# A matmul with rotary embedding: earlier turns of tiles 5 to 7, and other cuts of the last output units

## The chip, the cores and the metric

The kernel runs on one core of one Trainium2 chip. The metric is the device time of one execution in microseconds. The engines are TensorE (PE, with its weight loads listed as PEld), VectorE (DVE), ScalarE (ACT), GpSimd (POOL) and SyncE (SP), which here issues DMAs.

## The reference

For x of 16 x 512 x 768, a weight of 768 x 768, and cos and sin of 512 x 64, all float32, with 12 heads of 64:

```
y = matmul(x, weight).reshape(batch, seq, 12, 64)
y1, y2 = y[..., :32], y[..., 32:]
out1 = y1 * cos[:, :32] - y2 * sin[:, :32]
out2 = y2 * cos[:, 32:] + y1 * sin[:, 32:]
out = concatenate([out1, out2], -1).reshape(batch, seq, 768)
```

## The kernel before, in words

The 16 x 512 rows make 64 tiles of 128 rows, counted from 0 in this document. Four tiles make a group; there are 16 groups, 0 to 15 (`LAST` is 15). A group's output has 4 x 768 = 3072 columns and fills six PSUM banks of 512 columns (`py`, keys `ps0` to `ps5`). Two more banks (`pt`, two buffers) take the transposes.

A tile goes through these steps. SP loads it (`load`, L205) into one of ten buffers `xs`. ACT casts it to float16 (`cast`, L185, one of five buffers `xc`). PE turns it, that is, transposes it chunk by chunk into `pt`, and ACT copies `pt` into SBUF (`xt`, L185 again). There are two kinds of turn: `turn` (L251) uses one `pt` buffer and six transposes of 128 x 128; `turn_rows` (L266) turns the two halves of the partitions apart, twelve transposes of 64 x 64, and uses both `pt` buffers. From the first tile of the main loop on, `turn_rows` is used until near the end. Ten pairs of tiles in groups 5 to 14 (`BLOCKS`) are instead turned by DVE, some of them loaded by POOL's DMA queue.

Group 0 is computed chunk by chunk as the weights arrive (`mm0`, L333). In groups 1 to 14 the contraction is cut into two row halves that run on PE side by side (`walk`, `both`, `one`, L358): half 0 visits the three banks of a pair of tiles in the order 0, 1, 2 and half 1 in the order 2, 0, 1, each a lag of 1024 columns behind; so bank 0 is finished first, then bank 2, and bank 1 last. The last group uses whole matmuls again (L333), unit by unit.

A finished unit of columns goes to `rope`: DVE multiplies it from PSUM with cos and with the signed sin (L410) into two product rows, and POOL adds these, with halves exchanged, into the output buffer `ov` (L427). Up to group 13's first half POOL adds 1536 columns at once; afterwards unit by unit. The last two units of 256 are added by DVE itself, after all its products. Stores (L448) go out over ACT's or SP's queue.

`units(g)` says how a group's columns are cut: 512, 1024, 512, 1024 up to group 14; in group 15 three units of 512 and six of 256, the last two of which lie in the `pt` banks. The order of all this is written out by hand and each engine works in that order; waits are derived from which tile is read and written (`Flow.do`). Calls of `casts`, `turns`, `bturns`, `pool_loads` in the main loop say how far ahead of the matmuls a tile is cast and turned (`C_AHEAD`, `T_AHEAD`). `pump`, called after each cast, issues the next loads.

Around the start of the main loop the order is: the matmuls of tile 3 (its chunks 0 to 2), turn 4, cast 6, chunks 3 to 5 of tile 3, the last product of group 0, turn 5; then, in the loop, group 1 by `both`, with turn 6, casts 7 and 8, turn 7 at the end of the step of tile 5, and cast 9.

Of the kernel before, what the change touches and what calls it, by code (L numbers as in the profile page):

```python
# [16 lines left out]
class Flow:  # L17
# [24 lines left out]
    def do(self, e, make, reads=(), writes=(), dma=None, tick=True, after=0):  # L42
        need = {}
        for k in reads:
            for s, v in self.wrote.get(k, {}).items():
                need[s] = max(need.get(s, 0), v)
        for k in writes:
            for d in (self.wrote, self.readby):
                for s, v in d.get(k, {}).items():
                    need[s] = max(need.get(s, 0), v)  # L50
        if e == "pe":
            need.pop("pe", None)
            if after:
                need["pe"] = after
        waits = self.settle(e, need)
        for s, v in waits[:-1]:
            self.eng[e].wait_ge(self.sem(s), v)
        i = make(self.eng[e])
        if waits:
            s, v = waits[-1]  # L60
            i.wait_op(self.sem(s), v, "sem-ge")
        name, step = (dma, 16) if dma else (e, 1)
        self.sem(name)
        at = self.count[name] + step
        if tick or dma:
            i.then_inc(self.sems[name], step)
            self.count[name] = at
            self.known[name, at] = dict(self.seen[e])
        for k in reads:
            d = self.readby.setdefault(k, {})  # L70
            d[name] = max(d.get(name, 0), at)
        for k in writes:
            self.wrote[k] = {name: at}
            self.readby[k] = {}
        return i
# [30 lines left out]
def kernel(  # L106
# [23 lines left out]
    QB = 4  # L130
    NG = B * SB // QB
    NTILE = QB * NG
    CHUNKS = [(t, e) for t in range(NT) for e in range(2)]
    LAST = NG - 1
# [28 lines left out]
    def products(at, n, lo, hi):  # L163

        mem, base, name = (tq_mem, at, "tq") if at < 6144 else (w_flat, at - 6144, "tw")
        keys = {f"{name}{c // 256}" for j in range(2)
                for c in range(base + j * n + lo, base + j * n + hi, 256)}
        v = mem[:, base : base + 2 * n].rearrange("p (j n) -> p j n", j=2)
        return v[:, :, lo:hi], sorted(keys)
# [3 lines left out]
    py = nc.alloc_psum_tensor("py", [P, 6 * 512], FP32).ap()  # L173
# [4 lines left out]
    def ring(name, n, state={}):  # L178
        k = state.get((id(f), name), 0)
        state[id(f), name] = k + 1  # L180
        return k % n
# [118 lines left out]

    def units(g):
        if g < LAST:
            return [(c, z, py[:, c:z], [f"ps{b}" for b in range(c // 512, z // 512)], "pool")
                    for c, z in ((0, 512), (512, 1536), (1536, 2048), (2048, 3072))]
        u = [(c, c + 512, py[:, c : c + 512], [f"ps{c // 512}"], "pool")
             for c in range(0, 1536, 512)]
        if g == LAST:
            for k, (home, bank) in enumerate([
                (py[:, 1536:1792], "ps3"), (py[:, 0:256], "ps0"),
                (py[:, 2048:2304], "ps4"), (py[:, 2560:2816], "ps5"),  # L310
                (pt_b[0][:, 0:256], "pt0"), (pt_b[1][:, 0:256], "pt1"),
            ]):
                c = 1536 + 256 * k
                u.append((c, c + 256, home, [bank], "pool" if k < 4 else "dve"))
        return u

    def pieces(g, s):
# [51 lines left out]
    at = [0, LAG]  # L369
# [22 lines left out]
    def rope(g, u):  # L392
        c0, c1, ps, banks, adder = u
        w, r = c1 - c0, g % SB
        nh = w // D
        whole = 0 < g < LAST - 1 and (g, c0 // 1536) != (LAST - 2, 1)
        if adder == "dve":
            k = len(late)
            tq, keys = xs_b[k][:, 0 : 2 * w].rearrange("p (j n) -> p j n", j=2), [f"xs{k}"]
        elif 0 < g < LAST:  # L400
            lo = c0 % 1536
            if lo == 0:
                tq_of[0] = HOMES[ring("tq", len(HOMES))]
            tq, keys = products(tq_of[0], 1536, lo, lo + w)
            if tq_of[0] >= 6144:
                keys = keys + W_HOME
        else:
            homes = HOMESL if g else HOMES0
            tq, keys = products(homes[ring(f"tq{g}", len(homes))], w, 0, w)
        do("dve", lambda eng: eng.tensor_tensor(  # L410
            out=tq.rearrange("p j (h d) -> p j h d", d=D),
            in0=ps.rearrange("p (h d) -> p h d", d=D)
            .unsqueeze(1).broadcast_to((P, 2, nh, D)),
            in1=csn[:, :, r, :].unsqueeze(2).broadcast_to((P, 2, nh, D)),
            op=MULT), reads=banks + ["csn"], writes=keys)
        if g not in ov_of:
            ov_of[g] = ring("ov", NOV)
        o = ov_of[g]

        if whole:  # L420
            if c0 % 1536 == 0:
                return
            c0, w = c0 - 512, 1536
            tq, keys = products(tq_of[0], 1536, 0, 1536)

        def add():
            do(adder, lambda eng: eng.tensor_tensor(  # L427
                out=ov_b[o][:, ds(c0, w)].rearrange("p (h t d) -> p h t d", t=2, d=HD),
                in0=tq[:, 0].rearrange("p (h t d) -> p h t d", t=2, d=HD),
                in1=tq[:, 1].rearrange("p (h t d) -> p h t d", t=2, d=HD)[:, :, ::-1, :],  # L430
                op=ADD), reads=[q for q in keys if q not in W_HOME], writes=[f"ov{o}c{c}" for c in range(c0, c1, 64)])

        if adder == "dve":
            late.append(add)
        else:
            add()
# [77 lines left out]
    def mm0(i, c):  # L514
        last = c == CHUNKS[-1]
        ps = pieces(0, i)
        for p in ps:
            a, z, _, bank = p
            stop = last and (z % 512 == 0)
            mm_piece(i, p, c, False, stop, tick=last or p is ps[-1])  # L520
# [44 lines left out]
    def casts(upto, most=NTILE):  # L565
        while state["cast"] < min(upto, NTILE) and most > 0:
            most -= 1
            i = state["cast"]
            state["cast"] += 1
            if not is_block(i):  # L570
                castx(i, "act")
            elif i % 2 == 0 and BLOCKS[pair_of(i)] == "sp":
                cast_pair(pair_of(i))
                xb_used[0] += 1
            pump()

    def turns(upto, most=NTILE):
        while state["turn"] < min(upto, NTILE) and most > 0:
            i = state["turn"]
            state["turn"] += 1  # L580
            if not is_block(i):
                most -= 1
                (turn_rows if rows_on[0] else turn)(i, "act")
# [19 lines left out]
    for g in range(LAST):  # L603
        for h in (0, 2):
            i = QB * (g + 1) + h
# [5 lines left out]
            elif g < LAST - 2:  # L611
                i = QB * (LAST - 2) + 2 * (g - LAST + 4) + h // 2
# [2 lines left out]
            stores.setdefault(i, []).append(q)  # L615

    C_AHEAD, T_AHEAD, B_AHEAD, P_AHEAD = 5, 3, 4, 20
    SETTLED = 2 * QB

    for i in (0, 1):  # L620
        mm0(i, CHUNKS[5])
# [5 lines left out]
    for c in CHUNKS[:3]:  # L627
        mm0(3, c)
    turns(5)
    casts(7)  # L630
    for c in CHUNKS[3:]:
        mm0(3, c)
    rope(0, U0[3])
    turns(6)

    for i in range(QB, NTILE):
        g, s = divmod(i, QB)
        us = units(g)
        done_to = (s + 1) * H
        rows_on[0] = QB <= i < QB * LAST - 1  # L640
        if g < LAST:
            if s % 2 == 0:
                for r in range(2):
                    lines[r].extend(walk(i // 2, r))
            for n in range(1, 4):
                both((i - QB) * 4608 + n * 1536)
                if n == 1 and i > QB + 1:
                    turns(i + T_AHEAD, 1)
        if i == QB * LAST:
            both(NTILE * 4608)  # L650
        for p in pieces(g, s) if g == LAST else ():
            a, z, _, bank = p
            for c in CHUNKS:
                mm_piece(i, p, c, c == CHUNKS[0], c == CHUNKS[-1],
                         tick=c == CHUNKS[-1])
            for u in us:
                if u[1] == z:
                    rope(g, u)
        bturns(i + B_AHEAD)
        turns(i + 1 + (T_AHEAD if i > QB + 1 else 2), 1)  # L660
        casts(i + 1 + (C_AHEAD if i >= SETTLED else 4), 2 if i == QB else 1 + i % 2)
        pool_loads(i + P_AHEAD)
        for q in stores.get(i, ()):
            store(*q)
        if g == LAST:
            if s == 2:
                store(g, 0, H, "sp")
            if s == 3:
                store(g, H, 2 * H, "act")
# [4 lines left out]
    for k, add in enumerate(late):  # L674
        c = 3 * H + 256 + 256 * k
# [38 lines left out]
```

## Time and profile before

| what | value |
|---|---|
| median of 3 runs | 153.49 us (153.34 to 154.13) |
| the profiled execution | 154.31 us |
| its span in the trace | 152.5 us |
| DMA | 51.27 MB, 336 GB/s in the mean |
| PE's granted clock | 1.00 until 140 us, 0.87 in the stretch after |

The span is the time between the first and the last event in the trace; the execution's own time has 1.8 us around it. Busy lines give the engine, its busy time and share, and its number of instructions. In a timeline line come the start, the length, the engine, the line of code, the operation with output and input tiles, shapes and count, and in brackets the idle time just before and what ended it. "DVE tq" and "DVE w_raw" are products, in one of two places in memory. A wait for several semaphores is put down to the one that came last by the profile, which can be another than the one really needed.

### The profile page before, as it was taken

How to read it: one execution, taken by the hardware profiler on the slowest of the kernel's cores; microseconds unless marked ns; L12 is line 12 of the kernel's file. 1: busy time of each engine (PE TensorE's matmuls, PEld its weight loads, DVE VectorE, ACT ScalarE, POOL GpSimd, SP SyncE). 2: the span in 40 equal slices, each digit the busy share in tenths (PEclk: the TensorE clock that was granted, in tenths of full speed). 3: DMA queues.
4: the chain of work that ended last, by engine and by line, in shares of the span. 5: the costliest groups of instructions: out<-in, count | busy, mean ns of one | idle time of the engine just before them, and what ended most of it. 6: DMA issues, size and time to landing. Idle time of an engine off the chain costs nothing.

```text
span 152.5 us, 4394 instructions
## 1 busy us (share of the span) xinstructions
PE 141.1 (93%) x1944; PEld 116.9 (77%) x1944; DVE 126.4 (83%) x92; ACT 77.5 (51%) x92; POOL 123.1 (81%) x68
## 2 busy tenths in 40 slices
PE   6869988999999999999999999999999999999910
PEld 2435656888888988888898888888888888876800
DVE  0245988588888889899989998999989998979990
ACT  3444749679877852648261906183345626362000
POOL 1000395899789997999999999999996979998990
PEclk9999999999999999999999999999999999999995
DMA  4999999999999999999999999999999999965474
GB/s 131 330 387 402 402 401 389 267 342 349 324 364 346 313 351 359 300 361 350 350 357 361 382 309 356 370 391 319 360 367 413 413 373 395 377 250 216 194 285 142
DMA packets 27555, 51.27 MB, mean 336 GB/s; under 512 B 7184, under 2 KB 13072, under 8 KB 27536
## 3 DMA queue, kind: packets, MB, share of 16 engines
q1 hardware_dynamic: 14592, 27.92, 53.5%
q10 hardware_dynamic: 7504, 21.10, 35.3%
q0 software_dynamic: 5440, 1.97, 10.4%
q8 instruction: 15, 0.25, 0.6%
q14 instruction: 4, 0.03, 0.1%
HBM read 27.79 MB, written 25.17 MB: 347 GB/s over the span
## 4 chain that ended last, share of the span: by engine, by line
PE 75%; DMA 5%; DVE 5%; POOL 4%; SPq 4%; issue 2%; ACT 2%; POOLq 0%; ACTq 0%; DVEq 0%
PE py L358 69%; DMA sin_sb<-in_sin_dram 5%; PE pt L266 5%; POOL ov L427 4%; DVE tq L410 3%; SPq L227 2%; DVE w_raw L410 2%; SPq L205 1%; ACT xc L185 1%; ACT xt L185 1%; POOLq L670 0%; SPq L464 0%; PE pt L251 0%; DVE csn L552 0%; DVE csn L554 0%
## 5 line engine op out<-in xcount | busy, mean ns | idle before, releaser
L427 POOL TENSOR_TENSOR ov<-tq 128x1536 f32<-128x1536 f32 (+3 forms) x31 | 76.6, 2487 | 19.7 <-DVE tq L410 19.7
L358 PE MATMUL py<-w_sb,xt 64*128 64x256 f16 (+1 forms) x864 | 81.9, 323 | 1.3 <-DVE tq L410 0.7
L410 DVE TENSOR_TENSOR tq<-py,csn 128x1024 f32<-128x1024 f32 (+2 forms) x47 | 74.6, 1622 | 6.4 <-PE py L358 6.2
L358 PEld LDWEIGHTS py<-w_sb,xt 64*128 64x128 f16 x864 | 62.7, 94 | 10.1 <-DVE tq L410 1.1
L185 ACT COPY xt<-pt 128x768 f16<-128x768 f16 x42 | 33.6, 800 | 53.0 <-PE pt L266 48.8
L358 PE MATMUL py<-w_sb,xp 64*128 64x512 f16 (+1 forms) x480 | 47.6, 323 | 0.0
L185 ACT CAST xc<-xs 128x768 f16<-128x768 f32 x44 | 38.7, 905 | 9.2 <-DMA xs<-in_x_dram 9.1
L410 DVE TENSOR_TENSOR w_raw<-py,csn 128x1024 f32<-128x1024 f32 (+1 forms) x20 | 35.0, 1751 | 5.1 <-PE py L358 5.0
L427 POOL TENSOR_TENSOR ov<-w_raw 128x1536 f32<-128x1536 f32 (+2 forms) x11 | 34.8, 3168 | 5.3 <-DVE w_raw L410 5.3
L358 PEld LDWEIGHTS py<-w_sb,xp 64*128 64x128 f16 x480 | 35.5, 94 | 4.5
L333 PE MATMUL py<-w_sb,xt 128*128 128x256 f16 (+1 forms) x96 | 15.5, 313 | 1.4 <-DVE w_sb L185 1.1
L266 PE MATMUL pt<-ident,xc 64*128 64x64 f16 x432 | 15.0, 190 | 0.0
L266 PEld LDWEIGHTS pt<-ident,xc 64*128 64x128 f16 x432 | 14.4, 95 | 0.8
L333 PEld LDWEIGHTS py<-w_sb,xt 128*128 128x128 f16 x96 | 8.7, 98 | 6.8 <-DVE w_sb L185 2.7
L220 POOL DMA_DIRECT2D xh<-in_x_dram x20 | 11.6, 588 | 0.0
L185 ACT CAST xd<-xb 128x1536 f16<-128x1536 f32 x5 | 8.2, 1636 | 0.0
L185 DVE CAST w_sb<-w_raw 128x768 f16<-128x768 f32 x6 | 3.3, 558 | 4.0 <-DMA w_raw<-in_weight_dram 4.0
L294 DVE STREAM_TRANSPOSE xp<-xh 128x768 f32<-128x768 f32 x5 | 6.2, 1236 | 0.0
L509 PE MATMUL py<-cold 128*128 128x512 f16 x12 | 4.9, 569 | 1.4 <-DVE cold L452 1.4
L185 DVE COPY xt<-pt 128x768 f16<-128x768 f16 x2 | 1.1, 558 | 5.2 <-PE pt L251 5.2
L251 PEld LDWEIGHTS pt<-ident,xc 128*128 128x128 f16 x48 | 3.2, 103 | 2.6 <-ACT xc L185 1.5
L294 DVE STREAM_TRANSPOSE xp<-xd 128x768 f32<-128x768 f32 x5 | 4.8, 968 | 0.0
(16 smaller groups left out, 14.4 us busy)
## 6 DMA issues: line engine op xcount, KB each, us to landing
out_dram<-ov ACTq DMA_DIRECT2D x26, 768.0 KB, 9.1
xs<-in_x_dram SPq DMA_DIRECT2D x44, 384.0 KB, 15.2
xb<-in_x_dram SPq DMA_DIRECT2D x20, 192.0 KB, 17.6
out_dram<-ov SPq DMA_DIRECT2D x4, 768.0 KB, 3.7
w_raw<-in_weight_dram SPq DMA_DIRECT2D x6, 384.0 KB, 7.6
xh<-in_x_dram POOLq DMA_DIRECT2D x20, 96.0 KB, 13.2
out_dram<-ov SPq DMA_DIRECT2D x1, 384.0 KB, 2.3
out_dram<-ov ACTq DMA_DIRECT2D x1, 384.0 KB, 2.3
```

What stands on the lines that cost most here:

```text
L185: eng.copy(out=o, in_=i_) if e == "act" else eng.tensor_copy(out=o, in_=i_)
L205: do(e, lambda eng: eng.dma_start(out=xs_b[k], in_=x[b].rearrange("(p r) h -> r p h", r=SB)[r]), writes=[f"xs{k}"], dma=f"xs{k}")
L220: do(e, lambda eng: eng.dma_start(out=dst[ts(q, R)], in_=src[r, q]), writes=[f"{name}q{q}"], dma=name)
L227: do(e, lambda eng: eng.dma_start(out=w_raw[:, t, h], in_=wv[t, h]), writes=[f"wr{t}{h}"], dma=f"w{t}{h}")
L251: do("pe", lambda eng: eng.transpose(pt[:, t, h, :], src[:, t, h, :], ident), reads=[f"xc{c}", "ident"], writes=[f"pt{k}"], tick=(t, h) == ...
L266: do("pe", lambda eng: eng.transpose(pts[r][:, t, h, :], src[rows, t, h, :], ident[rows, rows]), reads=[f"xc{c}", "ident"], writes=[f"pt{r ...
L294: do("dve", lambda eng: eng.transpose(out=dst, in_=src), reads=rd, writes=[f"xp{z}"])
L333: do("pe", lambda eng: eng.matmul(ps, get(t, h), w_sb[:, t, h, a - s * H : z - s * H], start=start, stop=stop), reads=[key, f"w{t}{h}"], w ...
L358: do("pe", lambda eng: eng.matmul(py[:, a:z], get(t, h)[rows], w_sb[rows, t, h, a - s * H : z - s * H], start=start, stop=not opens and en ...
L410: do("dve", lambda eng: eng.tensor_tensor(out=tq.rearrange("p j (h d) -> p j h d", d=D), in0=ps.rearrange("p (h d) -> p h d", d=D) .unsque ...
L427: do(adder, lambda eng: eng.tensor_tensor(out=ov_b[o][:, ds(c0, w)].rearrange("p (h t d) -> p h t d", t=2, d=HD), in0=tq[:, 0].rearrange(" ...
L509: do("pe", lambda eng: eng.matmul(py[:, ts(b, 512)], cold[:, 0:P], cold, start=True, stop=warmed[0] < WARM - 6), reads=["cold"], writes=[f ...
```

## The change

Three things. First, the order around the main loop's start: turn 5 moves ahead of tile 3's chunk 5; casts 6 and 7 follow group 0's last product; turn 6 stays at the end of the loop's first step, followed by cast 8 alone; turn 7 moves to the first third of the step of tile 5, and turn 8 takes the place at its end, followed by casts 9 and 10. Up to tile 14 each cast is then one step ahead of before; later the order is the same. Second, group 14's last unit of 1024 columns becomes two of 512, which `both` hands to `rope` as their banks are finished, bank 5 before bank 4. Third, group 15 has four units of 512 and four of 256: the columns 1536 to 2048 are one unit in bank 3 instead of two in banks 3 and 0. POOL adds the first six units, DVE the last two as before.

```
     def units(g):
         if g < LAST:
+            cut = [2560] if g == LAST - 1 else []
+            at = [0, 512, 1536, 2048] + cut + [3072]
             return [(c, z, py[:, c:z], [f"ps{b}" for b in range(c // 512, z // 512)], "pool")
-                    for c, z in ((0, 512), (512, 1536), (1536, 2048), (2048, 3072))]
+                    for c, z in zip(at, at[1:])]
         u = [(c, c + 512, py[:, c : c + 512], [f"ps{c // 512}"], "pool")
-             for c in range(0, 1536, 512)]
+             for c in range(0, 2048, 512)]
         if g == LAST:
             for k, (home, bank) in enumerate([
-                (py[:, 1536:1792], "ps3"), (py[:, 0:256], "ps0"),
                 (py[:, 2048:2304], "ps4"), (py[:, 2560:2816], "ps5"),
                 (pt_b[0][:, 0:256], "pt0"), (pt_b[1][:, 0:256], "pt1"),
             ]):
-                c = 1536 + 256 * k
-                u.append((c, c + 256, home, [bank], "pool" if k < 4 else "dve"))
+                c = 2048 + 256 * k
+                u.append((c, c + 256, home, [bank], "pool" if k < 2 else "dve"))
...
     turns(5)
-    casts(7)
-    for c in CHUNKS[3:]:
+    for c in CHUNKS[3:5]:
         mm0(3, c)
+    turns(6)
+    mm0(3, CHUNKS[5])
     rope(0, U0[3])
-    turns(6)
+    casts(8)
...
                 both((i - QB) * 4608 + n * 1536)
-                if n == 1 and i > QB + 1:
+                if n == 1 and i > QB:
                     turns(i + T_AHEAD, 1)
...
-        turns(i + 1 + (T_AHEAD if i > QB + 1 else 2), 1)
-        casts(i + 1 + (C_AHEAD if i >= SETTLED else 4), 2 if i == QB else 1 + i % 2)
+        turns(i + 1 + (T_AHEAD if i > QB else 2), 1)
+        casts(i + 1 + (C_AHEAD if i > QB else 4), 1 + i % 2)
```

More of the change, by code (lines that the diff above doesn't have):

```diff
@@ L617 @@
     C_AHEAD, T_AHEAD, B_AHEAD, P_AHEAD = 5, 3, 4, 20
-    SETTLED = 2 * QB
     for i in (0, 1):
```

## The prediction

> **What bounds the kernel now.** I read the page first: the busy shares and the chain that ended last.
>
> ```profile
> PE 141.1 (93%) x1944; PEld 116.9 (77%) x1944; DVE 126.4 (83%) x92; ACT 77.5 (51%) x92; POOL 123.1 (81%) x68
> PE 75%; DMA 5%; DVE 5%; POOL 4%; SPq 4%; issue 2%; ACT 2%; POOLq 0%; ACTq 0%; DVEq 0%
> ```
>
> PE is the bound from about 20 us on; the chain runs through its matmuls from 20.20 to 137.3 us, with one break by ACT near 22 to 25 us. After PE's last group it passes to DVE, POOL and a store. So a gain can come from PE's holes near the start or from the work after 137.3 us. Next I took the waits of PE alone, and the timelines of PE and ACT between 17 and 26 us.
>
> ```profile
> 18.27 0.50 PE L251 MATMUL pt<-ident,xc 128*128 128x128 f16 x6
> 18.73 0.80 PE L358 MATMUL py<-w_sb,xt 64*128 64x512 f16 x3
> 20.20 1.67 PE L358 MATMUL py<-w_sb,xt 64*128 64x512 f16 x16 [0.67 <-DVE tq L410]
> ...
> 24.01 0.73 PE L358 MATMUL py<-w_sb,xt 64*128 64x256 f16 x6
> 25.35 0.37 PE L358 MATMUL py<-w_sb,xt 64*128 64x512 f16 x1 [0.61 <-ACT xt L185]
> ```
>
> ```profile
> 18.46 0.89 ACT L185 CAST xc<-xs 128x768 f16<-128x768 f32 x1
> 19.25 0.81 ACT L185 COPY xt<-pt 128x768 f16<-128x768 f16 x1
> 22.09 0.80 ACT L185 COPY xt<-pt 128x768 f16<-128x768 f16 x1 [2.04 <-PE pt L266]
> 22.79 1.71 ACT L185 CAST xc<-xs 128x768 f16<-128x768 f32 x2
> ```
>
> I count tiles from 0. The four ACT lines are cast 6, copy 5, copy 6, and casts 7 and 8; copy 7 follows at 24.40 and ends at 25.21. There are two holes in PE. The second (0.61 by the profile) is the wait for copy 7, which stands behind casts 7 and 8 on ACT. The first is put down to DVE, but the first matmul of tile 5 needs bank 2, whose product (DVE's second) ended at 19.03, and copy 5, which ended at 20.06. Matmuls start 0.14 after the copy in both places (20.06 to 20.20, 25.21 to 25.35), so I read the first hole as ACT's too. Matmul ends are modelled, so I measure holes from starts: 512 columns are issued every 0.21, so the next start was due at 19.37 and came at 20.20 (0.83); at the second it was due at 24.57 and came at 25.35 (0.78).
>
> Last, the tail, from the timelines of DVE and POOL:
>
> ```profile
> 135.55 1.22 DVE L410 TENSOR_TENSOR w_raw<-py,csn 128x1024 f32<-128x1024 f32 x1 [0.27 <-PE py L358]
> 137.41 2.29 DVE L410 TENSOR_TENSOR w_raw<-py,csn 128x2048 f32<-128x2048 f32 x1 [0.63 <-PE py L358]
> ```
>
> ```profile
> 137.92 1.27 POOL L427 TENSOR_TENSOR ov<-w_raw 128x512 f32<-128x512 f32 x1
> 139.78 2.36 POOL L427 TENSOR_TENSOR ov<-w_raw 128x1024 f32<-128x1024 f32 x1 [0.58 <-DVE w_raw L410]
> 142.10 6.82 POOL L427 TENSOR_TENSOR ov<-tq 128x512 f32<-128x512 f32 x7
> ```
>
> DVE waits 0.63 for the last bank of group 14, POOL waits 0.58 for that product of 1024 columns, and then POOL works without a hole to 148.93. Its last store lands at 150.80; DVE's last store (add ended at 148.35) lands at 150.41.
>
> **The change, part by part, early.** All is rescheduled by hand with the durations of these rows; the order on each engine is read off the built instructions of both kernels.
>
> Turn 5 moves ahead of the last two matmuls of tile 3: its transposes start at 17.95 (cast 5 ended at 17.88) instead of 18.27, and copy 5 now precedes cast 6, so it starts when copy 4 leaves ACT, 18.48, and ends at 19.29. Tile 5's first matmul starts at 19.29 + 0.14 = 19.43: gain 0.77. Tile 3's two matmuls start 0.33 later; the product that needs them starts on DVE at 20.08 after others, so that costs nothing.
>
> Casts 6 and 7 follow on ACT: 19.20 to 20.09 and 20.00 to 20.90 (durations 0.89 and 0.90; loads landed at 17.95 and 18.91). Transposes 6 start at 21.52 - 0.77 = 20.75, and end at 21.28; copy 6 runs 21.32 to 22.12.
>
> Now the new wait. Transposes 7 stood at 23.75, 2.2 us behind those of tile 6; now they stand in front of the matmul of 22.44, due at 21.67. A half-row turn fills both pt buffers, so it needs copy 6 out: 22.12 plus 0.06 (cast 4's end at 16.89 to its transposes at 16.95) = 22.18. PE waits 0.51, and every matmul behind waits too, though tiles 4 and 5 are ready. That hole is not in the trace of before; its bounds are 0 (copy 6 leaves in time) and 0.51 + 0.9 (one more cast in front of copy 6); I take 0.51, nearest to the rows for the copy. The trace shows the same queueing at 24.74: the matmul of tile 7 waited and the ready matmuls of tile 6 behind it did not start. The Trainium skill says so as a rule that speaks against this move: in "TensorE: Matmul & The Clock Gate", Part 2, only weight loads are pulled ahead and the matmuls stay in program order. By that rule, which the trace bears out here, the hole is lost; if matmuls could pass, the early sum would be 0.5 larger.
>
> After that, copy 7: cast 8 runs 22.03 to 22.95 and copy 7 from 22.85 to 23.65. Transposes 8 are due at about 23.7 and need copy 7 at 23.65 + 0.06, so hardly any wait. Tile 7's first matmul is then due near 24.55 with its copy long done: the 0.78 hole goes. Sum: 0.77 - 0.51 + 0.78 = 1.04; I take 1.0. What is late next: transposes 9 are due near 26.0 and cast 9 ends at 25.86; transposes 10 and DVE's bank releases have over 0.5 us.
>
> Other work that moves: the loads keep their order on SP; that of tile 16 waits for cast 6 (0.7 later) and that of tile 17 for cast 7 (2.8 sooner), both behind a queue that delivers them after 29 us, so I cost them at nothing. The first store of group 0 falls behind one more cast on ACT; its data wait longer than that anyway. POOL's add at 27.09 does not move, and POOL, with POOL DMA issues behind it, gets its 1.0 back only by 40.9 us, where it now idles 0.85.
>
> That 1.0 must survive to 137 us. For it: between 30 and 136 us no wait of PE is listed, and DVE and POOL idle for PE's data again and again (POOL 0.79 at 58.48, 1.54 at 115.81). Against it: loads come at their own time. Casts at 103.87 and 112.81 began 0.02 after their loads; but their transposes stand at 109.67 and 117.82, over 4 us later. I keep the 1.0.
>
> **The tail**, in before's clock. Group 14's last unit of 1024 becomes two of 512. Bank 5 closes at 136.24, bank 4 at 137.30. DVE takes bank 5 at 136.81 (after the product that ends at 136.78) and bank 4 at 138.06, 1.22 each, done at 139.28 instead of 139.70. POOL then has no hole: adds at 137.92, 139.16, 140.39 and on to 141.63, where before it was at 142.10 (step 1.235, from 142.10, 143.33, 144.57). Splitting costs 2 x 1.235 against 2.36; the hole of 0.58 goes: 0.47. The last group's unit at 1536 is one of 512 instead of two of 256: 1.235 against 0.68 x 2 = 1.36, 0.12 more. POOL ends at 148.34 instead of 148.93.
>
> DVE gains less. Its 512 product at column 1536 needs six matmuls of 512 columns from 141.48 on, ended at 142.94; DVE, free at 142.58, waits and starts at 143.04 (before: 143.01, on the half of it). It runs 143.04 to 144.25, then four of 0.60 steps and the two late adds (0.88, 0.94): end 148.31 against 148.35. So PE takes the place of the removed hole, and DVE's last store, landing at 150.37, is now the last; before it was POOL's at 150.80. With the order of the final waits (the last test of a store at 150.93 becomes 150.40), the tail gives 0.53. Bounds: 0.4 (DVE starts 0.1 later) to 0.6 (POOL's own gain).
>
> **Sum.** 1.0 + 0.53, so 1.5. The profiled execution took 154.31 with a span of 152.5; it would be 152.8, span 151.0. It is 0.8 above the median of the runs, so from 153.49 I predict 152.0 us, 1.0% faster. A measurement of this kernel tells about 0.5% (0.77 us) from no change.
>
> **Rivals.**
> - *The early gain is lost* (only the tail): the waits of the turns for copies 6 and 7 take more, for example one cast more in front of each, 0.9 apiece, or loads pace the middle. For it: 0.51 is already lost by my own count, and transposes 8 and 9 have under 0.2 us. Against: every wait there is set by ACT, which has two idle stretches. 153.49 - 0.5 = 153.0. Chance 0.14.
> - *The tail gives nothing*: DVE's late start or a slower final add leaves its last store at 150.8. DVE's own gain is only 0.04, which speaks for it; that POOL's store was the last by 0.4 speaks against. 153.49 - 1.0 = 152.5. Chance 0.13.
> - *PE's new wait is hidden* (copy 6 leaves sooner, or PE's due time is later than I think): 151.5. Chance 0.06.
> - *Slower*: cast 7 now stands in front of copy 6 and waits there for its load. It landed at 18.91, 1.1 before the cast starts. If it comes later than 20.0 + 0.4 (ACT's idle time after cast 7), each us holds copy 6, transposes 7 and all matmuls behind by a us. It would have to land after 22.7 to undo 1.5 and add 0.77; loads landed at a step of 0.97 (15.97, 16.94, 17.95, 18.91), so that is four loads late: 154.4. Chance 0.07.
>
> My forecast has 0.60. Faster: 0.60 + 0.13 + 0.06, less 0.05 for the 152.5 case, which is close to the bound, = 0.74. Within 0.5%: 0.14 + 0.05 = 0.19. Slower: 0.07. The range of 151.3 to 153.0 reaches from the hidden wait (less 0.2 of spread) to the lost early gain.
>
> **What would show it.** Early: no hole of PE before 19.4 of over 0.1, a new one of about 0.5 near 21.7 before transposes of 64x64, put down to ACT, none near 25; transposes 8 to 10 about 1 us sooner from 26 us on, and the chain still on PE to about 136.3. If the hole near 21.7 is over 1 us, or PE lists waits after 30 us, the early step is wrong. Tail: POOL without a hole from group 14's adds to its end, about 0.6 sooner relative to PE's last matmul; DVE idle about 0.4 before its fourth product of the last group; DVE's last store landing last. If POOL still waits before group 14's last adds, the tail step is wrong.

## The result, and the profile after

| | before | changed |
|---|---|---|
| median | 153.81 us (153.34 to 154.46, 4 runs) | 151.88 us (151.79 to 152.49, 4 runs) |
| the profiled execution | 154.31 us, span 152.5 | 151.85 us, span 150.1 |

The ratio is 0.988, with a 95% interval of 0.983 to 0.993: the change is faster, by 1.9 us between the medians, where 1.5 was forecast. A later set of 12 executions of the same kernel was less even and gave half of this ("The changed kernel once more", below); ratios leave out executions more than 1.5% above the fastest of the same kernel.

The page after, busy line and chain:

```profile
PE 140.7 (94%) x1938; PEld 101.4 (68%) x1938; DVE 126.9 (85%) x92; ACT 77.9 (52%) x92; POOL 123.0 (82%) x68
PE 87%; DMA 4%; DVE 4%; SPq 1%; issue 1%; ACT 1%; DVEq 0%
```

PE is as busy as before (140.7 against 141.1 us) in a shorter span, and its share of the chain rose from 75% to 87%; POOL has left the chain. PE's timeline near the start (start, length, engine, line, operation, count, idle time before and what ended it):

```profile
18.11 2.37 PE L359 MATMUL py<-w_sb,xt 64*128 64x512 f16 x19
...
20.50 0.81 PE L359 MATMUL py<-w_sb,xt 64*128 64x512 f16 x8
21.57 0.35 PE L266 MATMUL pt<-ident,xc 64*128 64x64 f16 x12 [0.26 <-ACT xt L185]
21.75 1.47 PE L359 MATMUL py<-w_sb,xt 64*128 64x512 f16 x16
23.07 0.35 PE L266 MATMUL pt<-ident,xc 64*128 64x64 f16 x12
23.26 2.11 PE L359 MATMUL py<-w_sb,xt 64*128 64x512 f16 x23
```

Both old holes are gone, and one new one stands before the turn of tile 7. ACT in the same stretch:

```profile
17.18 1.49 ACT L185 COPY xt<-pt 128x768 f16<-128x768 f16 x2
18.57 1.72 ACT L185 CAST xc<-xs 128x768 f16<-128x768 f32 x2
20.71 0.80 ACT L185 COPY xt<-pt 128x768 f16<-128x768 f16 x1 [0.42 <-PE pt L266]
```

These are copies 4 and 5, casts 6 and 7, and copy 6, which ends at 21.51; the turn starts 0.06 later. The tail, from DVE and then POOL:

```profile
133.75 3.74 DVE L411 TENSOR_TENSOR w_raw<-py,csn 128x1024 f32<-128x1024 f32 x3 [0.28 <-PE py L359]
137.41 6.24 DVE L411 TENSOR_TENSOR tq<-py,csn 128x1024 f32<-128x1024 f32 x6
...
144.76 1.84 DVE L428 TENSOR_TENSOR ov<-xs 128x256 f32<-128x256 f32 x2
```

```profile
136.10 3.76 POOL L428 TENSOR_TENSOR ov<-w_raw 128x512 f32<-128x512 f32 x3
139.80 6.52 POOL L428 TENSOR_TENSOR ov<-tq 128x512 f32<-128x512 f32 x6
```

DVE's three products of group 14's second half and POOL's adds of them are now joined (no bracket, so no idle time before the second line). POOL ends at 146.31, DVE at 146.60.

**Where the 2.46 us between the two spans lie.** Three points of the trace divide them: PE's first matmul of the main loop (18.73 before, 18.11 after), its last (137.03, 135.21) and the span's end.

| stretch | before | after | difference |
|---|---|---|---|
| start to first main-loop matmul | 18.73 | 18.11 | -0.61 |
| first to last main-loop matmul | 118.31 | 117.10 | -1.21 |
| last main-loop matmul to the end | 15.50 | 14.85 | -0.65 |

The first row is not the change's: DVE's first product, before which nothing was moved, already starts at 15.01 instead of 15.61, because the loads landed sooner in that execution. (In two kernels below that keep the old order, `tail_only` and `split14_only`, the first main-loop matmul starts at 18.41 and 18.13.) Before's profiled execution was 0.5 above its median. The change's share is 1.21 + 0.65 = 1.86, which fits the 1.93 between the medians. The two lower rows are what the experiments are compared by, since they leave out the first loads.

### The profile page after: what moved, and what is told of

Same layout as the page of the kernel before. It is cut to its first block, busy times and chain, and to the rows that moved or that the text cites. A ratio compares the mean times of both kernels' runs of the same rounds, so it can differ in the third digit from the quotient of the medians.

```text
span 150.1 us, 4381 instructions
## 1 busy us (share of the span) xinstructions
PE 140.7 (94%) x1938; PEld 101.4 (68%) x1938; DVE 126.9 (85%) x92; ACT 77.9 (52%) x92; POOL 123.0 (82%) x68
## 4 chain that ended last, share of the span: by engine, by line
PE 87%; DMA 4%; DVE 4%; SPq 1%; issue 1%; ACT 1%; DVEq 0%
PE py L359 73%; PE py L334 8%; PE pt L266 4%; DMA w_raw<-in_weight_dram 4%; DVE tq L411 2%; PE pt L251 1%; DVE ov L428 1%; SPq L205 1%; SPq L227 1%; ACT xt L185 1%; DVE xs L411 0%; DVE w_sb L185 0%; SPq L710 0%; DVEq L57 0%; SPq L116 0%
## 5 line engine op out<-in xcount | busy, mean ns | idle before, releaser
L359 PE MATMUL py<-w_sb,xt 64*128 64x256 f16 (+1 forms) x864 | 80.7, 323 | 0.0
L359 PEld LDWEIGHTS py<-w_sb,xt 64*128 64x128 f16 x864 | 53.2, 94 | 17.8 <-DVE tq L411 0.4
L359 PE MATMUL py<-w_sb,xp 64*128 64x256 f16 (+1 forms) x480 | 46.8, 323 | 0.0
L428 POOL TENSOR_TENSOR ov<-w_raw 128x1536 f32<-128x1536 f32 (+1 forms) x12 | 35.0, 2926 | 3.6 <-DVE w_raw L411 3.4
L359 PEld LDWEIGHTS py<-w_sb,xp 64*128 64x128 f16 x480 | 30.4, 94 | 9.5
L334 PEld LDWEIGHTS py<-w_sb,xt 128*128 128x128 f16 x90 | 8.1, 98 | 7.2 <-DVE w_sb L185 2.7
L266 PE MATMUL pt<-ident,xc 64*128 64x64 f16 x432 | 12.3, 190 | 0.3 <-ACT xt L185 0.3
```

Of the source, the lines that this page charges most:

```text
L266: do("pe", lambda eng: eng.transpose(pts[r][:, t, h, :], src[rows, t, h, :], ident[rows, rows]), reads=[f"xc{c}", "ident"], writes=[f"pt{r ...
L334: do("pe", lambda eng: eng.matmul(ps, get(t, h), w_sb[:, t, h, a - s * H : z - s * H], start=start, stop=stop), reads=[key, f"w{t}{h}"], w ...
L359: do("pe", lambda eng: eng.matmul(py[:, a:z], get(t, h)[rows], w_sb[rows, t, h, a - s * H : z - s * H], start=start, stop=not opens and en ...
L428: do(adder, lambda eng: eng.tensor_tensor(out=ov_b[o][:, ds(c0, w)].rearrange("p (h t d) -> p h t d", t=2, d=HD), in0=tq[:, 0].rearrange(" ...
```

## The experiments

The theory is that of the prediction: PE's holes at copies 5 and 7 go, a smaller one comes before the turn of tile 7, and the tail loses POOL's hole. All times are compared with runs of the kernel before on the same chip.

**The two halves apart.** `early_only` has `units` as before; `tail_only` has only the new `units`.

> The early reordering alone, with the cuts of groups 14 and 15 as before. Holes theory (the gain is what PE no longer waits for copies 5 and 7, less its new wait before the turn of tile 7, 0.51): about 1.2 us faster than before, and the distance from PE's first matmul of L358 to its last as in the changed kernel. Rival (most of the early difference of the two profiles is that one execution's loads landed 0.6 sooner, which has nothing to do with the change): only 0.6 us faster.

> The new cuts of groups 14 and 15 alone, with the early order as before. Theory: 0.5 to 0.65 us faster than before; POOL without a hole from group 14's adds on, its end 0.6 to 0.8 nearer to PE's last matmul; the two early holes of PE stand as before. Rival (DVE's late start gives it all back, its own end being nearly where it was): within 0.1 us of before.

Measured: early alone, ratio 0.994 (0.991 to 0.997), middle stretch 117.11, tail 15.50. Tail alone, ratio 0.998 (0.996 to 0.999), middle stretch 118.31, tail 14.84. So the early order gives 1.20 and the cuts give 0.66; neither changes the other's stretch. By the stretches both theories stand. The times are less clear: by the medians the early order alone gave 0.9 (153.03 against 153.96), and its interval, 0.5 to 1.3 us, holds both the theory's 1.2 and the rival's 0.6; the cuts alone gave 0.47 (153.49), just under the 0.5 of their theory. Four of the nine executions of the early order lie above 153.1; the only one profiled took 152.49, so what slowed the others isn't shown.

**The first hole alone.**

```
     turns(5)
-    casts(7)
-    for c in CHUNKS[3:]:
+    for c in CHUNKS[3:5]:
         mm0(3, c)
-    rope(0, U0[3])
     turns(6)
+    mm0(3, CHUNKS[5])
+    rope(0, U0[3])
+    casts(7)
```

> Only the turn of tile 5 moves ahead of tile 3's last chunk, with its copy ahead of cast 6; casts 7 and 8 and the turns of tiles 6 to 8 stay as before. Holes theory: the first hole falls from 0.83 to under 0.1, the second stays at about 0.8 to 1.0, there is no hole before the turn of tile 7: 0.75 us faster than before. Rival (DVE, to which the profile put the first hole, ends it): no gain, the hole stays at the end of DVE's third product.

Measured: ratio 0.996 (0.994 to 0.998), 0.77 us between the medians; middle stretch 117.53, 0.78 less than before. PE's timeline:

```profile
18.41 2.37 PE L358 MATMUL py<-w_sb,xt 64*128 64x512 f16 x19
...
24.25 0.37 PE L358 MATMUL py<-w_sb,xt 64*128 64x512 f16 x1 [0.60 <-ACT xt L185]
```

The first hole is closed (nineteen matmuls in one run), the second stands. Tile 5's first matmul starts at 19.11, while DVE's third product runs from 18.63 to 19.85: so the profile's "DVE tq" in front of the first hole was the event that happened to come last, and the copy was what PE needed.

**What the new hole waits for.** `turn128` has `rows_on[0] = QB + 2 <= i < QB * LAST - 1`, so that tiles 6 to 8 are turned whole.

> The changed kernel, but tiles 6 to 8 are turned whole (six transposes of 128 x 128 into one pt buffer) instead of by halves. Theory (the hole before the turn of tile 7 is the wait for a pt buffer that copy 6 still reads): that turn finds the other buffer free, the hole goes; three turns of 0.33 instead of 0.19 cost 0.4 of that again: from PE's first matmul of L358 to its last 117.0 us (changed kernel 117.1, before 118.3). Rival (the turn waits for cast 7 or for ACT's order and not for the buffer): the hole of 0.5 stays and the distance is 117.5.

PE, then ACT, of this kernel:

```profile
20.20 0.51 PE L251 MATMUL pt<-ident,xc 128*128 128x128 f16 x6
20.64 0.82 PE L359 MATMUL py<-w_sb,xt 64*128 64x256 f16 x9
21.40 0.51 PE L251 MATMUL pt<-ident,xc 128*128 128x128 f16 x6
```

```profile
20.75 0.80 ACT L185 COPY xt<-pt 128x768 f16<-128x768 f16 x1 [0.67 <-PE pt L251]
```

The turn of tile 7 starts at 21.40, before copy 6 ends (21.55), with the other pt buffer; the hole is gone. So it was the buffer. The size I expected was wrong: the stretch is 117.76, not 117.0, longer than the changed kernel's. A whole turn costs PE 0.4 us more than one by halves, not 0.14 (three of them cost the 0.66 of the stretch and the 0.51 of the hole that went). The last matmul before such a turn starts 0.31 ahead of it (19.89 to 20.20) and the next one 0.44 after its start; in between neither half lane starts one. The rival's 117.5 is not far from the measured length, but its hole is not there.

**The new hole taken away.** `turn7_mid` moves the turns of tiles 7 and 8 by a third of a step, and casts 9 to 11 between the copies:

```
-                if n == 1 and i > QB:
+                if n == 1 and i > QB + 1:
                     turns(i + T_AHEAD, 1)
+                if n == 2 and i == QB + 1:
+                    turns(i + T_AHEAD, 1)
+                if n == 1 and i == QB + 2:
+                    casts(i + C_AHEAD, 1)
...
-        turns(i + 1 + (T_AHEAD if i > QB else 2), 1)
-        casts(i + 1 + (C_AHEAD if i > QB else 4), 1 + i % 2)
+        turns(i + 1 + (T_AHEAD if i > QB + 1 else 2), 1)
+        casts(i + 1 + (C_AHEAD if i > QB + 1 else 4), 1 if i < 2 * QB else 1 + i % 2)
```

> The changed kernel, but the turn of tile 7 stands a third of a step later, that of tile 8 a third of a step later too, and casts 9 to 11 come one at a time between the copies. Holes theory: copy 6 has left when the turn of tile 7 is due, so the new hole of 0.51 goes, and at most 0.15 comes back at the first matmul of tile 7: about 0.4 us faster than the changed kernel, 2.2 to 2.4 faster than before. Rival (the hole only moves on to the copies of tiles 7 and 8, since ACT is what is short there): within 0.1 us of the changed kernel.

Measured: no hole between 17 and 26 us, middle stretch 116.74, 0.36 less than the changed kernel. Ratio to before 0.988 (0.985 to 0.991). In the trace the theory holds; by the times (median 152.03) it can't be told from the changed kernel. Part of the gain is lost in this execution's tail, 15.04 against 14.85: DVE's two late adds took longer, which the next experiments explain.

**The tail's parts.** `split14_only` has only the split of group 14's last unit.

> Only the split of group 14's last unit, the last group as before. Theory (POOL's hole of 0.58 goes, and POOL's store is the one that lands last): from PE's last matmul of L358 to the span's end 15.0 to 15.1 us instead of 15.5, 0.4 to 0.5 us faster than before; DVE then waits for nothing in the last group and its end comes 0.35 to 0.4 sooner too. Rival (the last group's cut is what matters): 15.4 or more.

Measured: ratio 0.997 (0.996 to 0.999), tail 15.21, so 0.29 of the 0.65, less than I expected. POOL's hole is gone, but DVE's last two adds took 2.32 us instead of 1.75: the first of them 1.98 beside POOL's adds, the second 0.41 when POOL had ended. The last add is what the last store waits for, so it gave back part of what was gained. This is not owed to the old cut of the last group. With all the new cuts, too, the two adds come in two forms: 0.96 to 0.98 and 0.94 in the first profile, `tail_only` and `changed_again` (tail 14.84 or 14.85), but 1.63 to 1.68 and 0.41 in `turn7_mid`, `turn128`, `nx8` and `nx12` (tail 15.04 to 15.10), as in this line of `turn7_mid`:

```profile
144.01 1.97 DVE L428 TENSOR_TENSOR ov<-xs 128x256 f32<-128x256 f32 x2
```

So the cuts are worth 0.65 in one form and 0.40 to 0.46 in the other, and the 0.29 of the split alone, measured in the slower form, must be set beside the latter. What decides between the forms is not known. The next kernel takes the cause away; it starts from `turn7_mid`:

```
-                u.append((c, c + 256, home, [bank], "pool" if k < 2 else "dve"))
+                u.append((c, c + 256, home, [bank], "dve"))
...
-    store(LAST, 2048, 3 * H, "act")
-    store(LAST, 3 * H, 3 * H + 256, "act")
     for k, add in enumerate(late):
-        c = 3 * H + 256 + 256 * k
+        c = 2048 + 256 * k
         add()
-        store(LAST, c, c + 256, "sp")
+        store(LAST, c, c + 256, "act" if k % 2 == 0 else "sp")
```

> The kernel with the later turn of tile 7, and DVE adds all four last units of 256 after its products, so that POOL has ended when DVE adds. Theory (beside POOL's adds a DVE add of 256 takes 0.94, alone 0.41): four adds of 0.41 to 0.45, DVE's end within 0.2 us of the two-add version (11.3 to 11.5 us after PE's last matmul of L358), POOL's end 1.5 us earlier, time 0.0 to 0.2 us less than with the later turn alone. Rival (the add itself takes 0.9): four adds of 0.9, 1.7 us slower.

```profile
142.93 1.27 DVE L411 TENSOR_TENSOR xs<-pt,csn 128x512 f32<-128x512 f32 x2
144.13 1.42 DVE L428 TENSOR_TENSOR ov<-xs 128x256 f32<-128x256 f32 x4
```

Four adds take 1.42 us where two took 1.84 in the changed kernel: 0.41 each once POOL is silent. DVE ends 10.97 after PE's last main-loop matmul instead of 11.39, the tail is 14.76, 0.09 less than the better form of two adds and 0.28 less than in `turn7_mid`. Median 151.61, ratio to before 0.984 (0.981 to 0.987). Five of its six executions took 151.07 to 152.06, one 154.28.

**The changed kernel once more.**

> The changed kernel beside the others on one chip, since the chip and the time of a run's first loads move the times by some tenths: theory 1.8 us faster than before (1.2 early and 0.6 in the tail), 0.35 slower than the version with the later turn of tile 7 and DVE's four adds. Rival (a good part of the first difference was chance): 1.2 us faster or less.

Measured: median 153.31 against 154.20, 0.9 us less; ratio 0.993 (0.989 to 0.997). So the rival came: in this set the gain is half of what the first four executions showed. The times fall into two sets: six of 152.1 to 152.5, six of 154.1 to 155.3, which is no better than before. In the profiled execution, one of the second set, the tail is 14.85 again, but the middle stretch is 119.03, 1.93 more than in the first profile. Turn by turn the two executions stay 0.35 apart up to the turn at 97.83, and are 2.22 apart from 126.28 on. PE's lines with idle time between 95 and 120 us, and three of ACT's:

```profile
100.50 0.35 PE L266 MATMUL pt<-ident,xc 64*128 64x64 f16 x12 [0.38 <-ACT xt L185]
103.92 3.51 PE L359 MATMUL py<-w_sb,xt 64*128 64x512 f16 x40 [0.47 <-ACT xt L185]
117.97 0.35 PE L266 MATMUL pt<-ident,xc 64*128 64x64 f16 x12 [0.16 <-ACT xt L185]
```

```profile
98.83 0.92 ACT L185 CAST xc<-xs 128x768 f16<-128x768 f32 x1 [4.48 <-DMA xs<-in_x_dram]
...
107.35 0.92 ACT L185 CAST xc<-xs 128x768 f16<-128x768 f32 x1 [2.79 <-DMA xs<-in_x_dram]
...
116.31 0.91 ACT L185 CAST xc<-xs 128x768 f16<-128x768 f32 x1 [3.60 <-DMA xs<-in_x_dram]
```

ACT stands still for loads, copies come late, and PE waits for the copies. This is the rival "loads pace the middle". The stretches by engine, two of the quicker execution, then two of this one (the last two columns are DMA's busy share and GB/s):

```profile
50.00:80.00 30.00, 30.00 (x443) 22.83 (x440) 28.37 (x19) 14.76 (x17) 28.85 (x13) 1.00 1.12 351
80.00:110.00 30.00, 30.00 (x453) 22.71 (x449) 28.51 (x19) 15.10 (x17) 29.64 (x17) 1.00 1.11 359
```

```profile
50.00:80.00 30.00, 30.00 (x441) 22.70 (x439) 28.36 (x19) 14.53 (x17) 28.79 (x12) 1.00 1.12 340
80.00:110.00 30.00, 29.15 (x435) 22.11 (x433) 27.82 (x18) 14.73 (x17) 28.95 (x16) 1.00 1.12 342
```

The queues are as busy, but move 342 instead of 359 GB/s; a packet of 3072 bytes of the loads takes 148 ns in the mean there instead of 131, one of the stores 124 against 123. The loads are the cause and not the effect: from 50 to 80 us, where PE has not lost anything yet (busy for all 30.00), they are already slower, 340 against 351 GB/s, 148 against 135 ns a packet. The load of tile 33 is issued 0.84 sooner than in the first profile (48.13 against 48.97) and lands 4.97 later (71.48 against 66.51). Single late executions stand in other sets too (154.60 among twelve of `turn5_only`); they were not profiled.

**Are the loads issued too late?** The changed kernel with `NX` 12 and with `NX` 8 instead of 10:

> The changed kernel with 12 instead of 10 buffers for loaded tiles, so that the load of a tile waits for the cast 12 tiles back and is issued some 4 us sooner. Theory (in part of the changed kernel's executions loads come too late near 100 and 117 us, casts and turns wait, and PE loses 2 us there, 119.0 instead of 117.1 from its first matmul of L358 to its last): the casts' waits for loads after 20 us fall to near nothing, no execution shows 119, and the times keep together within 0.8 us about 151.9. Rival (transfers as a whole set the pace in those executions, whenever they are issued): executions near 154.2 stay, in a third or more of the runs.

> The changed kernel with 8 instead of 10 buffers for loaded tiles: loads are issued some 4 us later. Theory: the margin of the transposes behind their loads, some 4 us in the changed kernel, is gone in every execution: PE waits for tiles between 40 and 120 us in all of them, the distance from PE's first matmul of L358 to its last is 119 or more, the times 154 or more. Rival (the late executions come from elsewhere): distance 117.1 in the profile and times as in the changed kernel.

Measured: with 12 buffers six executions of 151.95 to 152.77, ratio 0.990 (0.988 to 0.992), stretch 117.11; casts still wait 9.4 us for loads in all (12.0 with 10 buffers in the first profile). With 8 buffers four executions of 152.08 to 152.40, ratio 0.989 (0.986 to 0.991), stretch 117.08, casts' waits 11.9. So the forecasts of my theory fail: two buffers less cost nothing. But the kernels did not do what I meant them to do. SP's issue of the load of tile 49, with 8 and with 10 buffers:

```profile
83.35 1.78 SPq L205 DMA_DIRECT2D xs<-in_x_dram  x1
83.27 1.97 SPq L205 DMA_DIRECT2D xs<-in_x_dram  x1
```

With 12 it stands at 82.93. From 50 to 97 us SP waits for no buffer in any of these profiles: the next issue follows 0.04 after the last, and an issue takes 0.45 to 5.55 us. So the buffer count moved issues only early on (tile 14's: 19.72, 16.31 and 12.80 with 8, 10 and 12), and whether an earlier issue in the middle would help stays untested. The load of tile 49 takes 20 us from issue to landing (83.3 to 103.3 in the first profile). What makes the transfers slower in some executions stays open. The even times don't show that the buffers help: these two kernels and the next ran on another chip than the uneven set, where the changed kernel with 10 buffers was not run, so the chip is a rival that nothing here rules out.

**All together.** `turn7_dve4_nx12`:

> The later turn of tile 7, DVE's four adds and 12 load buffers together. Theory: distance 116.7, tail 14.8, no execution over 152.5; median 151.2 to 151.5, 1.7 to 1.9% faster than before. Rival: as with 10 buffers, one execution in five or more over 153.5.

Measured: 151.56 to 151.93 in four executions, median 151.75 against 154.05 before, ratio 0.985 (0.983 to 0.988), stretch 116.75, tail 14.77. The two stretches came as forecast and no execution passed 152.5, but the median is above the 151.2 to 151.5 that I expected. By its two stretches it is 0.43 below the changed kernel in their sum, level with `turn7_dve4` (116.73 and 14.76, with 10 buffers); by the times it can't be told from either.

## Why the prediction was right

The holes and the wait were where the prediction put them. That 152.0 and 151.88 are so close is in part luck: the gain was 1.9 and not 1.5, and the median of before rose from 153.49 to 153.81 with a fourth run.

- *First hole, 0.77.* `turn5_only` measured 0.78. Reading it as ACT's, against the profile's label, was right.
- *New hole before the turn of tile 7, 0.51.* The last matmul before it starts at 20.95, the next was due at 21.06 and the turn came at 21.57: 0.51. The profile lists 0.26, since it counts from modelled ends. Turns 6, 7 and 8 stand where the reckoning put them, less the 0.6 of the loads: 20.14, 21.57 and 23.07 against 20.15, 21.58 and 23.1. The rival in which the wait is hidden did not come.
- *Second hole, 0.78.* This term was too small. The early stretch gave 1.21, so the second hole was worth, by subtraction, 1.21 - 0.78 + 0.51 = 0.94. I took one half lane, due at 24.57; the other was due at 24.45, and after the hole turn 8's twelve transposes spread over 0.35 (25.36 to 25.71), where the changed kernel's take 0.16 (23.07 to 23.23).
- *Tail, 0.53.* Measured 0.65 here, and 0.40 to 0.46 in the four profiles with the slower form of the late adds: the forecast lies between, and had not seen that the adds vary. DVE's fourth product of the last group waits for PE as forecast: it starts 6.01 after PE's last main-loop matmul, both as reckoned (143.04 - 137.03) and as measured (141.22 - 135.21). Reckoned from the usual step of 1.14 between products, the 0.4 that I expected before it is there in two parts: 0.16 before the third product and 0.22 before the fourth. DVE's own end came 0.08 later relative to PE, not 0.04 sooner; its last store landed 1.86 after that end (13.25 - 11.39), not 2.07 as before (13.38 - 11.31), and that made up for it. As forecast, DVE's store is now the last to land and POOL's is not.
- *The gain survives to the end.* True of the first profile and of half of the later executions; in the others, by the one that was profiled, loads ate 1.9 us. That the first four executions were all of the quick kind was not forecast; it was luck, or owed to something that was not tested, such as the chip. Of my rivals this was the one with 0.14, and I argued against it with margins of over 4 us between a cast and its turn. Those margins were of one execution; in the later one tile 49's load landed at 107.3, against 103.8 before and 103.3 in the changed kernel's first profile.

## What to carry to other kernels

A turn or copy that is moved ahead brings its buffer's wait with it: reckon, for the new place, when the last reader of that buffer ends, since in an in-order engine the wait is paid by all that stands behind. Where an engine's label names one of several releasers, look for the event that the instruction really needs, and measure holes from starts when ends are modelled. A gain won early on a bound engine is kept only as long as the transfers keep their margin; take that margin from several executions.

## What the runs showed of the hardware

An add of 128 x 256 float32 on DVE takes 0.41 us alone and 0.89 to 0.98 beside POOL's adds of the same kind; in five profiles the first of two took 1.63 to 1.98 and the second, after POOL's end, 0.41. POOL's own add takes 0.71 to 0.77, or 0.90 to 0.91. The Trainium skill, "SBUF — State Buffer", section "Who interferes with whom", states that a VectorE instruction with two SBUF inputs contends with a GpSimd instruction that reads SBUF; these runs agree, with a factor of 2 or more for DVE.

After the new hole the two half lanes of PE start their matmuls together (21.75 and 21.76, 21.97 and 21.97), where before they ran 0.09 to 0.13 apart (22.44, 22.53, 22.66, 22.75). The busy time of the weight loads falls from 116.9 to 101.4 us with it, as more of them overlap. It is 101 to 105 us in all profiles with this hole or with the whole turns of `turn128`, and 114 to 118 in the others, `turn7_mid` among them, whose middle stretch is shorter. The rate does not change, and turns of the steady part follow each other in 2.13 us in both.
